# Hybrid encoder on one core: how the 64x64 triangular inverses are put together from 32x32 blocks

## The chip, the cores and the metric

The kernel runs on one core of one Trainium2 chip. The metric is the device time of one execution in microseconds (us). Three runs of the kernel before took 1709.49, 1710.0 and 1717.93 us, median 1710.0. The core has a matrix engine (TensorE; PE in the profile, its weight loads PEld), a vector engine (DVE), an activation engine (ScalarE, ACT), GpSimd (POOL) and SyncE (SP), which here issues DMAs.

## The reference

Two layers over 512 tokens of width 1024. Each layer normalises, projects, runs three token mixers beside each other, projects back, and ends with a gated MLP:

```
h = rms_norm(x);  proj = h @ w_in[l]
y_att = attention_mixer(...)     # windowed attention, 6 heads
y_dn  = deltanet_mixer(...)      # gated DeltaNet, two directions, 6 heads, chunks of 64
y_rw  = rwkv_mixer(...)          # RWKV-7, two directions, 4 heads
x = x + concat(y_att, y_dn, y_rw) @ w_out[l]
x = x + conv_ffn(rms_norm(x))
```

The change is in one piece of the two recurrent mixers. In DeltaNet, each chunk of 64 tokens needs the solution with a unit triangular matrix:

```
a_mat = lower + eye(64)          # strictly lower part from k_beta k^T * decay
sol = triangular_solve(a_mat, rhs, lower=True, unit_diagonal=True)
```

The reverse direction gives an upper triangle. RWKV-7 is written in the reference as a scan over tokens; the kernel computes it in chunks of 64 as well, with a unit triangular matrix per chunk and head. The kernel forms the inverses themselves. With 64 = 32 + 32 rows, the inverse of a block triangle has the inverses of the two diagonal blocks on its diagonal, and beside them one coupling block: inverse of one diagonal block, times the coupling block of the matrix, times the inverse of the other, with a sign.

## The kernel before

All matrix work is float32 through the matrix engine. A large projection splits both operands into a high and a low part and does three products for each weight tile of 128x128 (lines 332, 333, 334, each 128x512); the raw tile comes by DMA (`wr`, line 318), ACT makes its high part (`wh`, line 321), POOL its low part (`wl`, line 322). The weights stream in once per layer through three buffers of each.

A scheduler builds every engine's queue: the program is written as generators, each step carries costs and due times, and the rows of the queues differ from the order of the code. Each engine then works through its queue in order. The large products 332 to 334 are laid between the small products of the mixers as fillers. The order is not written by hand, so an edit in one helper shifts fillers in other places.

`invert` and `invert_both` (from lines 391 and 422) compute the inverses of all 32x32 diagonal blocks on DVE, four blocks of 32 partitions at a time, and leave them in two tiles: `o1`, and its transpose `o2`, each with one 32x32 block per unit. A unit is one chunk of one head pair; partitions 0 to 63 and 64 to 127 hold the two members `h` of the pair.

`finish_inverse` (line 445) then completes the 64x64 matrices `mt[h..h+64, c, 0:64]`, where before its call one off-diagonal block holds the coupling. It is called once per layer for RWKV (line 1005, 32 units, in groups of 16) and twice per layer for DeltaNet (line 1036, 24 units each, groups of 16 and 8). In a group:

- line 455: product `py`, coupling block (32x32, the weights) times `o2`, two products per unit (h = 0, 64), into PSUM;
- line 457: two ACT copies of 32 partitions, PSUM to the tile `yt`;
- line 461: product `pw`, `yt` block (32x32, the weights) times `o1`;
- line 465: per 8 units two ACT copies of 32 partitions from PSUM into the off-diagonal blocks, with the sign;
- line 469: per 8 units four ACT copies of 32 partitions put `o1` on the diagonal.

A float32 product shows as two matmul records in the trace: 64 products of lines 455 and 461 each in RWKV and 96 each in DeltaNet per layer give 256 and 384 records of the two lines together. The matrices are read next by the scans: line 619 (RWKV) and line 806 (DeltaNet), with 64x64 weights. Around them stand DeltaNet's conv lines 691 to 696, attention's products 886, 903 and 907, the rotary step line 867 on DVE, and the transposes 410 and 411, which write `o1` and `o2`. At the kernel's start `late_params` issues on SP the late part of the constants (line 205, 128x1816), and POOL makes its first low parts (line 322).

Of the kernel before, what the change touches and what calls it, by code (L numbers as in the profile page):

```python
# [7 lines left out]
F32 = mybir.dt.float32  # L8
F32R = mybir.dt.float32r
I32 = mybir.dt.int32  # L10
AF = mybir.ActivationFunctionType
# [3 lines left out]
P = 128  # L15
# [21 lines left out]
def _const_array():  # L37

    cols = []

    def add(name, a):
        a = np.asarray(a, np.float32)
        full = np.zeros((P, a.shape[1]), np.float32)
        full[: a.shape[0]] = a
        at = sum(c.shape[1] for c in cols)
        CONSTS[name] = (at, a.shape[1])
        cols.append(full)

    i = np.arange(P)
    add("ones", np.ones((P, P)))  # L50
    freq = np.zeros((P, 1))
    inv = (np.float32(500000.0) ** (-np.arange(8, dtype=np.float32) / np.float32(8))).astype(np.float32)
    for h in (0, 64):
        freq[h : h + 8, 0] = inv
        freq[h + 8 : h + 16, 0] = inv
    add("freq", freq)
    add("absign", np.where(np.arange(24) < 12, 1.0, -1.0)[:, None])
    for name, v in (("eps", EPS), ("rweps", RW_EPS), ("one", 1.0), ("halfpi", math.pi / 2)):
        add(name, np.full((P, 1), v))
    hi32 = (i % 64 >= 32).astype(np.float32)  # L60
    add("m32", np.stack([hi32 - 1.0, -hi32], 1))
    add("ident", np.eye(P))
    add("bd1", (i[:, None] // 64 == i[None, :] // 64))
    rot = np.zeros((P, P))
    for h in (0, 64):
        for d in range(8):
            rot[h + d + 8, h + d] = -1.0
            rot[h + d, h + d + 8] = 1.0
    add("rot", rot)
    kk = np.arange(384)  # L70
    add("attm", np.where(np.abs(kk[None, :] - 128 - i[:, None]) <= 128, 0.0, NEG))
    s, t = (i % 64)[:, None], np.arange(64)[None, :]
    add("mb", -np.concatenate([s < t, s <= t], 1).astype(np.float32))
    add("mkf", np.concatenate([s < t, s <= t], 1))
    add("mkb", np.concatenate([s > 63 - t, s >= 63 - t], 1))
    add("dnm", np.concatenate([np.where(s <= t, 0.0, NEG), np.where(s >= t, 0.0, NEG)], 1))
    add("smask", np.repeat((np.arange(T) % CL != 0)[None], P, 0))
    sel = np.zeros((P, 24))
    for hh in range(2):
        for p in range(3):  # L80
            for d in range(2):
                n, head = hh * 12 + p * 2 + d, p * 2 + hh
                sel[32 * d + 6 * d + head, n] = -1.0
                sel[64 + 12 + 6 * d + head, n] = 1.0
                sel[32 * d + 6 * d + head, n + 6] = -1.0
    add("sel", sel)
    return np.concatenate(cols, 1)


_CONST = _const_array()  # L90


# [23 lines left out]
def trunk(tc, t, out):  # L116
    nc = tc.nc
    V, S, G, PE = nc.vector, nc.scalar, nc.gpsimd, nc.tensor
    mult, add, sub, mx, mn = ALU.mult, ALU.add, ALU.subtract, ALU.max, ALU.min
    ctx = ExitStack()  # L120
    cp = ctx.enter_context(tc.tile_pool(name="cp", bufs=1))
# [5 lines left out]
    def nm(s):  # L127
        uid[0] += 1
        return f"{s}{uid[0]}"
# [5 lines left out]
    def ps(stream, shape=(P, T)):  # L135
        return psp.tile(list(shape), F32, tag="ps" + stream, bufs=PS_BUFS[stream], name=nm("ps"))
# [4 lines left out]
    def t2(stream, *free, dt=F32):  # L141
        return bp.tile([P, *(free or (T,))], dt, tag="t" + stream, bufs=T_BUFS[stream], name=nm("t" + stream))
# [31 lines left out]
    def C(name):  # L174
        a, n = CONSTS[name]
        return cst[:, a : a + n]

    ident, bd1, ones = C("ident"), C("bd1"), C("ones")
# [24 lines left out]

    def late_params():
        nc.sync.dma_start(cst[:, n0:], t["consts"][:, n0:])
        nc.sync.dma_start(par_all[:, :, n1:], t["params"][:, :, n1:])
        for l in range(DEPTH):
            nc.sync.dma_start(sinkb[l], t["attn_sink"][l].unsqueeze(0).broadcast_to([P, 6]))
# [22 lines left out]
    exp_ln_tables()  # L231

    pair_sq = cp.tile([P, 2, 32, 32], F32, name="pair_sq")


    cos_t, sin_t = fixed[:, W + DEPTH * NPAR : W + DEPTH * NPAR + T], fixed[:, W + DEPTH * NPAR + T : W + DEPTH * NPAR + 2 * T]
# [207 lines left out]

    def finish_inverse(st, o1, o2, units, upper, sign):

        ra, rb = (0, 32) if upper else (32, 0)
        n = len(units)
        for g0 in range(0, n, 16):
            grp = units[g0 : g0 + 16]  # L450
            py = ps(st)
            yt = t2(st, 16, 32)
            for i, (p, mt, c) in enumerate(grp):
                for h in (0, 64):
                    PE.matmul(py[h + rb : h + rb + 32, 32 * i : 32 * i + 32], mt[h + ra : h + ra + 32, c, rb : rb + 32], o2[h + ra : h + ra + 32, p, :], start=True, stop=True)  # L455
            for h in (0, 64):
                S.activation(yt[h + rb : h + rb + 32, : len(grp), :], py[h + rb : h + rb + 32, : 32 * len(grp)].rearrange("q (p c) -> q p c", c=32), AF.Copy)
            pw = ps(st)
            for i, (p, mt, c) in enumerate(grp):
                for h in (0, 64):  # L460
                    PE.matmul(pw[h + ra : h + ra + 32, 32 * i : 32 * i + 32], yt[h + rb : h + rb + 32, i, :], o1[h + rb : h + rb + 32, p, :], start=True, stop=True)  # L461
            for i in range(0, len(grp), 8):
                mt = grp[i][1]
                for h in (0, 64):
                    S.activation(mt[h + ra : h + ra + 32, :, rb : rb + 32], pw[h + ra : h + ra + 32, 32 * i : 32 * i + 256].rearrange("q (p c) -> q p c", c=32), AF.Copy, scale=sign)
        for i in range(0, n, 8):
            p, mt, _ = units[i]
            for h in range(0, P, 32):
                S.activation(mt[h : h + 32, :, h % 64 : h % 64 + 32], o1[h : h + 32, p : p + 8, :], AF.Copy)


    def token_shift(l, o, i, rb, dst):
# [439 lines left out]
    def layer(l, norm, xd, last):  # L912
# [9 lines left out]
        for i in range(8):  # L922
            o = proj(l, parts, COL_RW + P * i)
            if i == 0 and l == 0:
                derive_params()
            token_shift(l, o, i, rb, rkv[i // 2][:, i % 2, :])
            if i == 2 and l == 0:
                late_params()
            if i == 3:
                wau = bp.tile([P, 2, 256], F32, tag="wau", name=nm("wau"))  # L930
                nc.sync.dma_start(wau[0:64], t["rw_w_up"][l].rearrange("d r c -> r d c"))
                nc.sync.dma_start(wau[64:128], t["rw_a_up"][l].rearrange("d r c -> r d c"))
                gup = bp.tile([P, T], F32, tag="gup", name=nm("gup"))[:, :256]
                nc.sync.dma_start(gup, t["rw_g_up"][l])
# [68 lines left out]
        qkv.append(dn_proj(1))  # L1003
        o1, o2 = run(invert(rw["dpk"], True, V, t2("r")))
        finish_inverse("r", o1, o2, [(8 * u + c, rw["gb"][u], c) for u in range(4) for c in range(NCH)], True, 1.0)
        ap = attn_proj()
        heads = []
# [27 lines left out]
        for d in range(2):  # L1035
            finish_inverse("d", *inv[d], [(8 * p + c, dn["rm"][p][d], c) for p in range(3) for c in range(NCH)], d == 0, -1.0)
# [115 lines left out]
```

## Time and profile before

| | |
|---|---|
| runs of the kernel before | 1709.49, 1710.0, 1717.93 us |
| profiled execution, its own time | 1722.8 us |
| its span in the trace | 1721.0 us |
| mean granted TensorE clock | 0.931 |
| busy PE / PEld / DVE / ACT / POOL | 90 / 70 / 57 / 46 / 37% |
| copies of lines 457, 465, 469 | 24, 40, 80 |

The span is what the trace covers, from the first to the last instruction; 1.8 us of the execution's time lie around it. The profiled execution took 12.8 us more than the median of the three runs. A busy PE is counted from modelled ends of its instructions, which overlap, so the distance between two starts is the better price of a small product. The granted clock is given in parts of full speed, 1.0 for 2.4 GHz and 0.50 for 1.2 GHz.

### The profile page before, as it was taken

How to read it: one execution, taken by the hardware profiler on the slowest of the kernel's cores; microseconds unless marked ns; L12 is line 12 of the kernel's file. 1: busy time of each engine (PE TensorE's matmuls, PEld its weight loads, DVE VectorE, ACT ScalarE, POOL GpSimd, SP SyncE). 2: the span in 40 equal slices, each digit the busy share in tenths (PEclk: the TensorE clock that was granted, in tenths of full speed). 3: DMA queues.
4: the chain of work that ended last, by engine and by line, in shares of the span. 5: the costliest groups of instructions: out<-in, count | busy, mean ns of one | idle time of the engine just before them, and what ended most of it. 6: DMA issues, size and time to landing. Idle time of an engine off the chain costs nothing. (4 is left out here: it accounts for less than half of the span.)

```text
span 1721.0 us, 29049 instructions
## 1 busy us (share of the span) xinstructions
PE 1544.2 (90%) x11500; PEld 1208.7 (70%) x11500; DVE 973.5 (57%) x1595; ACT 792.0 (46%) x1493; POOL 638.7 (37%) x510
## 2 busy tenths in 40 slices
PE   7988889569999999999998887983899999999997
PEld 4676666347778888888876666652677788888885
DVE  6578946875535557731136797579563555555001
ACT  5547453355444444433336654351734544444321
POOL 4321323101265554445552112420104555555553
PEclk9989979669999999999999998995799999999998
DMA  6221211100143333333442012220003333333331
GB/s 185 73 57 38 56 38 44 37 2 20 36 122 96 98 98 95 96 104 114 119 101 68 25 45 50 55 70 1 4 19 93 102 95 97 98 99 114 101 101 65
DMA packets 230536, 126.07 MB, mean 73 GB/s; under 512 B 23656, under 2 KB 221416, under 8 KB 230400
## 3 DMA queue, kind: packets, MB, share of 16 engines
q1 hardware_dynamic: 228624, 121.02, 25.0%
q10 hardware_dynamic: 1776, 3.20, 0.6%
q8 instruction: 90, 1.47, 0.3%
q14 instruction: 46, 0.38, 0.1%
HBM read 117.84 MB, written 6.34 MB: 72 GB/s over the span
## 5 line engine op out<-in xcount | busy, mean ns | idle before, releaser
L322 POOL TENSOR_TENSOR wl<-wr,wh 128x512 fp32r<-128x512 f32 (+1 forms) x408 | 553.6, 1363 | 753.2 <-ACT wh L321 664.2
L332 PE MATMUL ps<-hh,wh 128*128 128x512 f32 x1248 | 505.2, 405 | 22.1 <-ACT wh L321 19.6
L333 PE MATMUL ps<-hl,wh 128*128 128x512 f32 x1248 | 504.5, 404 | 0.0
L334 PE MATMUL ps<-hh,wl 128*128 128x512 f32 x1248 | 500.9, 401 | 0.4 <-POOL wl L322 0.4
L321 ACT ACTIVATE wh<-wr 128x512 fp32r<-128x512 f32 (+1 forms) x408 | 246.2, 615 | 330.8 <-PE ps L333 262.4
L332 PEld LDWEIGHTS ps<-hh,wh 128*128 128x128 f32 x1248 | 237.8, 191 | 80.9 <-ACT wh L321 20.4
L333 PEld LDWEIGHTS ps<-hl,wh 128*128 128x128 f32 x1248 | 238.0, 191 | 56.8 <-issue 4.2
L334 PEld LDWEIGHTS ps<-hh,wl 128*128 128x128 f32 x1248 | 237.5, 190 | 56.8 <-issue 3.9
L1104 DVE TENSOR_TENSOR p<-ps,p 128x512 f32<-128x512 f32 x16 | 11.1, 692 | 196.6 <-PE ps L334 196.6
L332 PE MATMUL ps<-p,wh 128*128 128x512 f32 x256 | 99.6, 389 | 0.0
L333 PE MATMUL ps<-p,wh 128*128 128x512 f32 x256 | 99.6, 389 | 0.0
L334 PE MATMUL ps<-p,wl 128*128 128x512 f32 x256 | 99.6, 389 | 0.0
L903 PE MATMUL ps<-fixed,cv 128*128 128x128 f32 x120 | 24.9, 340 | 62.4 <-DVE cv L900 62.0
L1081 DVE TENSOR_TENSOR tr<-ps,rb 128x512 f32<-128x512 f32 x44 | 30.4, 691 | 80.9 <-PE ps L334 80.8
L292 POOL TENSOR_TENSOR tr<-tr,tr 128x512 f32<-128x512 f32 x32 | 42.6, 1332 | 70.4 <-ACT tr L285 59.9
L903 PEld LDWEIGHTS ps<-fixed,cv 128*128 128x128 f32 x120 | 16.0, 168 | 72.5 <-issue 44.8
L1084 DVE SCALAR_TENSOR_TENSOR td<-tr,fixed,td 128x511 f32<-128x511 f32 x44 | 42.8, 972 | 37.7 <-ACT td L1083 37.7
L285 ACT ACTIVATE tr<-p 128x512 f32<-128x512 f32 x36 | 22.6, 628 | 85.9 <-DVE p L1104 64.4
L791 POOL TENSOR_TENSOR sm<-sm,fixed 128x384 f32<-128x384 f32 x12 | 10.8, 896 | 121.5 <-DVE sm L820 64.5
L333 PEld LDWEIGHTS ps<-p,wh 128*128 128x128 f32 x256 | 48.1, 188 | 10.1
L332 PEld LDWEIGHTS ps<-p,wh 128*128 128x128 f32 x256 | 48.1, 188 | 10.1
L1084 DVE SCALAR_TENSOR_TENSOR tr<-td,fixed,tr 128x511 f32<-128x511 f32 x44 | 33.9, 771 | 37.5 <-ACT tr L1083 37.5
(294 smaller groups left out, 2559.7 us busy)
## 6 DMA issues: line engine op xcount, KB each, us to landing
wr<-ffn_w_up SPq DMA_DIRECT2D x176, 256.0 KB, 2.8
wr<-w_in SPq DMA_DIRECT2D x88, 256.0 KB, 2.9
wr<-ffn_w_down SPq DMA_DIRECT2D x80, 256.0 KB, 2.9
wr<-w_in SPq DMA_DIRECT2D x24, 128.0 KB, 2.4
p<-scr ACTq DMA_DIRECT2D x12, 256.0 KB, 3.5
wr<-w_out SPq DMA_DIRECT2D x32, 96.0 KB, 2.6
wr<-w_out SPq DMA_DIRECT2D x16, 192.0 KB, 2.9
p<-xt SPq DMA_DIRECT2D x8, 256.0 KB, 5.0
```

The source lines that it names most:

```text
L285: S.activation(sq, xk, AF.Square)
L292: G.tensor_tensor(acc, self.acc, sq, add)
L321: S.activation(hi[:, :n, :], raw[:, :n, :], AF.Copy)
L322: G.tensor_tensor(lo[:, :n, :], raw[:, :n, :], hi[:, :n, :].bitcast(F32), sub)
L332: PE.matmul(o, wh, xh, start=k == 0, stop=False)
L333: PE.matmul(o, wh, xl, start=False, stop=False)
L334: PE.matmul(o, wl, xh, start=False, stop=k == n - 1)
L791: G.tensor_tensor(gs, state, flat(gl, step), mult)
L903: PE.transpose(pp[:, P * j : P * j + P], scs[g][:, P * j : P * j + P], ident)
L1081: V.tensor_tensor(u, o, nf.rb, mult)
L1084: V.scalar_tensor_tensor(a[:, 1:], u[:, :-1], w(0), a[:, 1:], mult, add)
L1104: V.tensor_tensor(x1[j], o, x1[j], add)
```

## The change

The two products of a unit get weights of 64 columns in place of 32, so that each writes 64 partitions and its output lies on all 128 partitions for the pair. For `py` the weights are the whole rows of the coupling block, `mt[..., 0:64]`; the half of the output that comes from the other columns is not read. For `pw` the weights are `pair`: the block Y beside an identity block, so that the one product gives the whole block column (Y part times `o1`, and `o1` itself beside it). Y lies in a new tile `fin` (128 partitions, 33 blocks of 32), its odd slots; the even slots hold identities, written once by four POOL copies in `late_params`. The copies then go over all 128 partitions: one per group from `py` to `fin` with the sign, and per 8 units one of `o1` with a mask per partition (two more columns of the constant `m32`, zero on one half) and one of `pw`. `fin` is one tile for all groups, both mixers and both layers. Lines after the edit are 3 or 4 higher: 332 to 334 are 336 to 338, 867 is 870.

```
-    add("m32", np.stack([hi32 - 1.0, -hi32], 1))
+    add("m32", np.stack([hi32 - 1.0, -hi32, 1.0 - hi32, hi32], 1))
...
         nc.sync.dma_start(cst[:, n0:], t["consts"][:, n0:])
+        for h in range(0, P, 32):
+            G.tensor_copy(fin[h : h + 32, 0::2, :], ident[h : h + 32, h : h + 32].unsqueeze(1).broadcast_to([32, 17, 32]))
...
+    fin = cp.tile([P, 33, 32], F32, name="fin")
...
+        mask = C("m32")[:, 2 + ra // 32 : 3 + ra // 32]
...
+            s0 = 0
             py = ps(st)
-            yt = t2(st, 16, 32)
...
-                    PE.matmul(py[h + rb : h + rb + 32, 32 * i : 32 * i + 32], mt[h + ra : h + ra + 32, c, rb : rb + 32], o2[h + ra : h + ra + 32, p, :], start=True, stop=True)
-            for h in (0, 64):
-                S.activation(yt[h + rb : h + rb + 32, : len(grp), :], py[h + rb : h + rb + 32, : 32 * len(grp)].rearrange("q (p c) -> q p c", c=32), AF.Copy)
+                    PE.matmul(py[h : h + 64, 32 * i : 32 * i + 32], mt[h + ra : h + ra + 32, c, 0:64], o2[h + ra : h + ra + 32, p, :], start=True, stop=True)
+            S.activation(fin[:, 2 * s0 + 1 : 2 * (s0 + len(grp)) : 2, :], py[:, : 32 * len(grp)].rearrange("q (p c) -> q p c", c=32), AF.Copy, scale=sign)
             pw = ps(st)
             for i, (p, mt, c) in enumerate(grp):
+                at_i = 2 * (s0 + i) + (0 if upper else -1)
+                pair = fin.rearrange("p a b -> p (a b)")[:, 32 * at_i + 32 : 32 * at_i + 96]
                 for h in (0, 64):
-                    PE.matmul(pw[h + ra : h + ra + 32, 32 * i : 32 * i + 32], yt[h + rb : h + rb + 32, i, :], o1[h + rb : h + rb + 32, p, :], start=True, stop=True)
+                    PE.matmul(pw[h : h + 64, 32 * i : 32 * i + 32], pair[h + rb : h + rb + 32, :], o1[h + rb : h + rb + 32, p, :], start=True, stop=True)
             for i in range(0, len(grp), 8):
-                mt = grp[i][1]
-                for h in (0, 64):
-                    S.activation(mt[h + ra : h + ra + 32, :, rb : rb + 32], pw[h + ra : h + ra + 32, 32 * i : 32 * i + 256].rearrange("q (p c) -> q p c", c=32), AF.Copy, scale=sign)
-        for i in range(0, n, 8):
-            p, mt, _ = units[i]
-            for h in range(0, P, 32):
-                S.activation(mt[h : h + 32, :, h % 64 : h % 64 + 32], o1[h : h + 32, p : p + 8, :], AF.Copy)
+                p, mt, _ = grp[i]
+                S.activation(mt[:, :, ra : ra + 32], o1[:, p : p + 8, :], AF.Copy, scale=mask)
+                S.activation(mt[:, :, rb : rb + 32], pw[:, 32 * i : 32 * i + 256].rearrange("q (p c) -> q p c", c=32), AF.Copy)
```

New lines: `py` 461, its copy 462, `pw` 468, the masked copy of `o1` 471, the copy of `pw` 472, the identities 207. The scheduler lays some instructions otherwise than before, here at three places.

PE's queue before, layer 1, where RWKV's inverses are completed (`p_621`, `p_646`, `p_1160`, `p_1185` are the four matrix tiles `mt`):

```order
L334 MATMUL ps_2247<-hh_143,wl_2257 128x512
L455 MATMUL ps_1618<-p_1615,p_621 32x32 x16
L455 MATMUL ps_1618<-p_1615,p_646 32x32 x16
L461 MATMUL ps_1654<-p_1614,tr_1619 32x32
L455 MATMUL ps_1691<-p_1615,p_1160 32x32 x16
L455 MATMUL ps_1691<-p_1615,p_1185 32x32 x5
L461 MATMUL ps_1654<-p_1614,tr_1619 32x32 x31
L455 MATMUL ps_1691<-p_1615,p_1185 32x32 x11
L461 MATMUL ps_1727<-p_1614,tr_1692 32x32
```

The same place in the changed kernel:

```order
L338 MATMUL ps_2334<-hh_98,wl_2339 128x512
L461 MATMUL ps_1623<-p_1620,p_626 64x32 x16
L461 MATMUL ps_1623<-p_1620,p_651 64x32 x16
L336 MATMUL ps_2334<-hh_108,wh_2338 128x512
L337 MATMUL ps_2334<-hl_109,wh_2338 128x512
L338 MATMUL ps_2334<-hh_108,wl_2339 128x512
L336 MATMUL ps_2334<-hh_114,wh_2338 128x512
L337 MATMUL ps_2334<-hl_115,wh_2338 128x512
L338 MATMUL ps_2334<-hh_114,wl_2339 128x512
L336 MATMUL ps_2334<-hh_123,wh_2345 128x512
L468 MATMUL ps_1657<-p_1619,fin 64x32 x32
L461 MATMUL ps_1694<-p_1620,p_1165 64x32 x16
```

Six products of the next projection (`ps_2334`) stand ahead of the first `py`, seven between the first `py` and the first `pw`, and four between the second pair; before there were none. When the scan's first step (line 619, now 622) is through, 19 of them are done in place of 11.

DVE's queue before, at the same place (`tr_2184` is the rotary step on the projection's result, which frees its PSUM buffer):

```order
L404 TENSOR_TENSOR p_1551<-p_1551,tr_1550 128x2x29
L403 TENSOR_TENSOR tr_1550<-p_1551 128x30
L404 TENSOR_TENSOR p_1551<-p_1551,tr_1550 128x30
L410 STREAM_TRANSPOSE p_1614<-p_1551 128x32x32
L411 STREAM_TRANSPOSE p_1615<-p_1551 128x32x32
L867 SCALAR_TENSOR_TENSOR tr_2184<-ps_2146,rb_88 128x512
```

In the changed kernel the rotary step stands ahead of the last steps of the inverse:

```order
L408 TENSOR_TENSOR p_1556<-p_1556,tr_1555 128x7x24
L870 SCALAR_TENSOR_TENSOR tr_2169<-ps_2131,rb_89 128x512
L407 TENSOR_TENSOR tr_1555<-p_1556 128x150
L699 TENSOR_TENSOR cv_2012<-cv_2012,td_2020 128x512
L408 TENSOR_TENSOR p_1556<-p_1556,tr_1555 128x6x25
```

So the buffer that the six fillers write is free before the transposes, and the transposes come one instruction later.

PE's queue before, layer 1, where DeltaNet's inverses are completed (the second direction, `p_1881`, `p_2691`, `p_2780`):

```order
L461 MATMUL ps_3305<-p_3141,td_3270 32x32 x31
L455 MATMUL ps_3342<-p_3142,p_2780 32x32 x16
L334 MATMUL ps_3620<-hh_97,wl_3624 128x512
L332 MATMUL ps_3620<-hh_107,wh_3623 128x512
L333 MATMUL ps_3620<-hl_108,wh_3623 128x512
L334 MATMUL ps_3620<-hh_107,wl_3624 128x512
L461 MATMUL ps_3362<-p_3141,td_3343 32x32
L332 MATMUL ps_3620<-hh_113,wh_3623 128x512
L461 MATMUL ps_3362<-p_3141,td_3343 32x32 x15
L806 MATMUL ps_3439<-p_1921,p_1880 64x64 x2
```

And in the changed kernel:

```order
L468 MATMUL ps_3272<-p_3126,fin 64x32 x32
L461 MATMUL ps_3309<-p_3127,p_2765 64x32 x16
L338 MATMUL ps_3573<-hh_92,wl_3577 128x512
L336 MATMUL ps_3573<-hh_98,wh_3576 128x512
L337 MATMUL ps_3573<-hl_99,wh_3576 128x512
L338 MATMUL ps_3573<-hh_98,wl_3577 128x512
L468 MATMUL ps_3327<-p_3126,fin 64x32 x16
L809 MATMUL ps_3392<-p_1906,p_1865 64x64 x2
```

From the first `py` to the end of the scan's first step there were 12 fillers and are now 6; the small pieces of one kind set between two fillers, or fillers set singly into a row of small products, go from 6 to 3. In RWKV they go from 4 to 5.

At the start of the program SP issues the late constants behind three loads of raw weights in place of six, and POOL's queue is, after the change:

```order
L326 TENSOR_TENSOR wl_165<-wr_83,wh_164 128x512
L326 TENSOR_TENSOR wl_217<-wr_214,wh_216 128x512
L207 COPY fin<-fixed 32x17x32 x4
L326 TENSOR_TENSOR wl_223<-wr_220,wh_222 128x512
L326 TENSOR_TENSOR wl_259<-wr_256,wh_258 128x512
```

The four copies of identities stand between the third and the fourth weight's low part; before, nothing stood there.

## Rows read from the trace of the kernel before

**Rows 1.** The page: busy time by engine, and PE's granted clock over 40 slices.

```profile
PE 1544.2 (90%) x11500; PEld 1208.7 (70%) x11500; DVE 973.5 (57%) x1595; ACT 792.0 (46%) x1493; POOL 638.7 (37%) x510
PEclk9989979669999999999999998995799999999998
```

**Rows 2.** Stretches: start:end, us; busy us of PE, PEld, DVE, ACT, POOL; clock; DMA.

```profile
220.00:228.70 8.70, 6.16 (x201) 5.71 (x201) 1.24 (x3) 6.21 (x14) 0.00 (x0) 0.50 0.01 4
228.70:238.10 9.40, 9.40 (x85) 6.09 (x84) 0.00 (x0) 5.89 (x15) 1.27 (x1) 0.50 0.08 28
238.10:310.00 71.90, 70.74 (x852) 49.16 (x853) 48.42 (x83) 30.00 (x61) 27.36 (x31) 0.99 0.21 59
368.80:391.70 22.90, 21.04 (x437) 15.96 (x437) 6.80 (x15) 19.30 (x48) 0.00 (x0) 0.65 0.01 3
391.70:440.00 48.30, 45.55 (x807) 35.70 (x808) 31.78 (x100) 23.74 (x67) 8.37 (x8) 0.98 0.07 18
```

**Rows 3.** PE's timeline, RWKV: start, us, instruction, [idle before, releaser].

```profile
211.06 0.39 PE L333 MATMUL ps<-hl,wh 128*128 128x512 f32 x1
211.28 0.39 PE L334 MATMUL ps<-hh,wl 128*128 128x512 f32 x1
220.07 1.92 PE L455 MATMUL ps<-p,p 32*32 32x32 f32 x64 [8.40 <-DVE p L411]
222.68 0.26 PE L461 MATMUL ps<-p,tr 32*32 32x32 f32 x1 [0.69 <-ACT tr L457]
227.82 0.31 PE L461 MATMUL ps<-p,tr 32*32 32x32 f32 x2 [1.78 <-ACT tr L457]
...
232.66 0.63 PE L332 MATMUL ps<-hh,wh 128*128 128x512 f32 x1
233.09 0.63 PE L333 MATMUL ps<-hl,wh 128*128 128x512 f32 x1
233.65 0.48 PE L619 MATMUL ps<-p,p 64*64 64x64 f32 x4
234.06 0.79 PE L334 MATMUL ps<-hh,wl 128*128 128x512 f32 x1
234.65 0.63 PE L332 MATMUL ps<-hh,wh 128*128 128x512 f32 x1
```

**Rows 4.** PE's timeline, DeltaNet's inverses and scan.

```profile
379.12 1.20 PE L455 MATMUL ps<-p,p 32*32 32x32 f32 x63
388.56 1.54 PE L806 MATMUL ps<-p,p 64*64 64x64 f32 x22
...
407.32 0.92 PE L806 MATMUL ps<-sm,p 64*64 64x64 f32 x24 [0.67 <-DVE sm L802]
408.97 0.82 PE L903 MATMUL ps<-fixed,cv 128*128 128x128 f32 x6
410.10 1.25 PE L907 MATMUL ps<-tr,at 128*64 128x128 f32 x12
```

**Rows 5.** PE's timeline, a product with 12 moving columns.

```profile
112.82 0.61 PE L723 MATMUL ps<-fixed,td 128*64 128x12 f32 x14 [1.23 <-DVE td L367]
```

**Rows 6.** DVE's timeline, end of RWKV's 32x32 inverses.

```profile
218.13 1.89 DVE L411 STREAM_TRANSPOSE p<-p 128x1024 f32<-128x1024 f32 x1
219.90 0.65 DVE L867 SCALAR_TENSOR_TENSOR tr<-ps,rb 128x512 f32<-128x512 f32 x1
```

**Rows 7.** Groups by line, ACT: count | busy us, mean ns | idle before, releasers.

```profile
L469 ACT ACTIVATE p<-p 32x256 f32<-32x256 f32 x80 | 33.1, 414 | 17.9 <-DVE p L410 13.8 <-DVE p L440 3.0
L465 ACT ACTIVATE p<-ps 32x256 f32<-32x256 f32 x40 | 15.0, 375 | 5.1 <-PE ps L461 4.2
```

**Rows 8.** Start of the program: POOL's and PE's timeline.

```profile
19.11 2.86 POOL L322 TENSOR_TENSOR wl<-wr,wh 128x512 fp32r<-128x512 f32 x2
23.26 1.31 POOL L322 TENSOR_TENSOR wl<-wr,wh 128x512 fp32r<-128x512 f32 x1 [1.29 <-DMA wr<-w_in]
...
31.41 0.39 PE L334 MATMUL ps<-hh,wl 128*128 128x512 f32 x1
```

## The prediction

> **What bounds the kernel now.** I read the page first. PE is busy 90% of the span, ACT 46%, and the clock row stands at 9 in most slices, with dips in those where the mixers' small products run [rows 1]. Then the windows around the edit, in layer 1 [rows 2]. In the two stretches that follow the inverses, PE is busy 70.74 of 71.9 us and 45.55 of 48.3 us: whatever ACT saves there, PE has no gaps from which it could be paid back. The inverses' own stretches look different. RWKV's, 220.0 to 228.7, has PE at 6.16 of 8.70 us and ACT at 6.21, at clock 0.50. DeltaNet's, 368.8 to 391.7, has PE at 21.04 of 22.90 and ACT at 19.30, at 0.65. Last I read PE's timeline in those stretches for what ends each wait [rows 3]: 8.40 us on the DVE transpose, then 0.69 and 1.78 us on the ACT copies from `py`. So only two things count: PE time added or taken, and these few idle microseconds.
>
> **ACT's copies.** Before, 24 copies of line 457, 40 of 465 and 80 of 469. The last two cost 15.0 and 33.1 us [rows 7], and line 457 about 24 x 0.5 = 12 us more (its width is up to twice that of line 465's 0.375 us). After: 12, 20 and 20 copies of all partitions, at most 0.5 us each by the same rows (an ACT copy is priced there by its width, 0.375 to 0.414 us for 256), together about 24 us. ACT sheds some 36 us in the program. I put this at nothing by itself: it is off the path, apart from the waits counted below.
>
> **The products.** Their number is unchanged, 256 records per layer in RWKV and 384 in DeltaNet. Each now loads 64 weight columns in place of 32 and moves 32 as before. The price is the interval between starts. 32x32: (1.92 - 0.24) / 63 = 26.7 ns at clock 0.50 [rows 3], (1.20 - 0.19) / 62 = 16.3 ns at full clock [rows 4]. The trace has no 64x32. The bounds are unchanged (26.7 and 16.3), and 64x64: (1.54 - 0.32) / 21 = 58 ns slow, about 30 ns fast ((0.92 - 0.2) / 23 = 31) [rows 4]. To choose between them I looked for what the price follows. Fast, the 128*64 with 128 moving columns costs (1.25 - 0.28) / 11 = 88 ns, the 128*128 with 128 moving (0.82 - 0.26) / 5 = 112 ns [rows 4]: 0.46 and 0.44 ns for each column, loaded and moved together. Where products alternate between two row groups, as here (h = 0, 64), it is half: 32 + 32 gives 14 (measured 16.3), 64 + 64 gives 29 (about 30). By that 64 + 32 costs 1.5 times the old, 40 ns slow and 24.5 fast. RWKV runs slow: 256 x 13.3 = 3.4 us. DeltaNet about half and half: 384 x (13.3 + 8.2) / 2 = 4.1 us. Together **+7.5 us a layer**.
>
> The Trainium skill, "TensorE: Matmul & The Clock Gate", section "LDWEIGHTS (loading the stationary operand)", says that a load takes time by its number of columns, not of rows: 64 columns would take twice what 32 do. It speaks against the change, and by it alone the sum would be that of the second rival below, not this one. The trace agrees in part: a 128*64 product that moves only 12 columns still costs (0.61 - 0.206) / 13 = 31 ns [rows 5], so the load does count, yet the rows above make it one of two terms.
>
> **Idle time that goes.** RWKV's two waits on copies, 0.69 + 1.78 [rows 3], have fillers in them now. In DeltaNet's stretch PE is idle 22.90 - 21.04 = 1.86 us [rows 2]. Late next is the copy into `fin` in DeltaNet's first group, where `pw` follows `py` with no filler between: one full copy and its semaphores, which I put at 0.9 us (line 457's waits of 0.69 and 1.78 stand on both sides of it). 0.69 + 1.78 + 1.86 - 0.9 = **-3.4 us a layer**. Bounds: 0 if new waits eat it all, -4.3 if none appears. `fin` is one tile, so the second group's copy waits for the first group's `pw`; in PE's order that `pw` comes before the second `py` is through, so nothing is queued behind it.
>
> **Six fillers in the gap before RWKV's first `py`.** They go where PE sits idle 8.40 us, and cost nothing there; elsewhere they were 6 x 0.22 us, the distance of lines 333 and 334 [rows 3], 1.3 us. For it the rotary step, 0.65 us [rows 6], runs ahead of DVE's last steps and delays the transposes, on which `py` waits. 0.65 - 1.3 = **-0.65 us a layer**.
>
> **Small pieces between fillers.** A small piece set between two fillers costs more than its own time. From 233.09: 0.56 to the piece, 0.41 from it, 0.59 to the next filler [rows 3], against 2 x 0.43 for the fillers alone and 4 x 0.058 for the piece: 1.56 - 0.86 - 0.23 = 0.47 us. RWKV has one more (+0.47), DeltaNet three fewer (-1.4): **-0.9 us a layer**.
>
> **Fillers between clocks.** A filler takes 0.43 us at 0.50 [rows 3] and 0.22 at full clock. RWKV does 19 - 11 - 6 = 2 more in the slow stretch (+0.4), DeltaNet 6 fewer, half of them slow (-0.6): **-0.2 us a layer**.
>
> **The start.** Four copies on POOL stand ahead of the fourth low part. The first use of such a part that could be late is at 31.41 us, and it takes 1.31, so it must begin by 30.1; POOL ends the third at 21.97 [rows 8]. The 8.1 us between are 2.0 for each copy; the nearest row is the low part itself, 2.86 / 2 = 1.43 us for 512 columns (a copy has 544). I take 0, hidden behind products that are already fed. The constants now go ahead of the raw weights of the later parts; with 7.1 us of delay the slack would be used up, so the bounds are 0 and 2 us, once.
>
> **Sum.** 7.5 - 3.4 - 0.65 - 0.9 - 0.2 = +2.35 us a layer, +4.7 in two (layer 2 repeats the stages). The profiled execution took 1722.8 us (span 1721.0 and 1.8 around it) and would take 1727.5. The runs' median is 12.8 lower: 1727.5 - 12.8 = 1714.7, forecast **1715**.
>
> **Rivals.**
> (a) The wider load hides fully, and the price stays at 26.7 and 16.3. For it: loads of PE run beside products, PEld is busy 70% [rows 1]. Against it: rows 4 and 5, where loaded columns count. Then 2.35 - 7.5 = -5.15 a layer, -10.3 in two: 1700.
> (b) The 64-column load sets the pace, as if the product were 64x64. RWKV 256 x 31.3 = 8.0, DeltaNet 384 x (31.3 + 13.7) / 2 = 8.6, together 16.6 in place of 7.5: +11.45 a layer, +22.9: 1733. It is slower, and decides from about 43 ns a record at the slow clock (the sum's 40 and 3.8 us in two layers). For it: row 5's 31 ns with 12 columns moving. Against it: those weights have 128 rows and follow each other on the same rows.
> (c) The clock in DeltaNet. A mean of 0.65 in 22.90 us [rows 2] is about 30% at full clock, 6.9 us, with PE at 0.92 of it. With six fillers fewer the full-clock part may not come: 6.3 us a layer more, 1715 + 12.6 = 1728.
> (d) The clock in RWKV the other way. It was 0.50 from the first `py` on, after 8.40 us of idle. With six fillers in the gap, and eleven standing among the inverses' products where none stood, it may rise sooner: half of the 18.1 us from 220.0 to 238.1 [rows 2] is 9, of which I take 7, since waits don't shrink; 1715 - 14 = 1701.
> (e) The saved ACT time counts in full where ACT set the pace in the inverses' stretches: ACT 6.21 of 8.70 and 19.30 of 22.90. The idle time above is all that PE could win by it, so this is in the sum already.
>
> **How the numbers follow.** A measurement of this kernel can tell about 0.5%, 8.5 us: faster is below 1701.5, slower above 1718.5. Forecast (1705 to 1722): 0.46. (a) 0.23, (b) 0.16, (c) 0.08, (d) 0.07. Below 1701.5 lie most of (a) and half of (d), and little of the forecast: 0.27. Above 1718.5 lie (b), (c) and an edge of the forecast: 0.29. Between: 0.44. The range goes from just under (a) to just under (b), 1697 to 1731, which leaves out half of (b) and the tails; the forecast's own range is 1705 to 1722.
>
> **What would show it.** In the profile after: records of lines 461 and 468 at about 40 ns from start to start in RWKV (27 speaks for (a), 58 for (b)). ACT's lines 462, 471 and 472 at 24 us together. PE's idle before the first `pw` in RWKV gone, and the wait for DVE's transposes below 8.40. DeltaNet's first `pw` waiting about 0.9 us for its copy. POOL's low parts at the start late with no PE wait behind them. PE busy as before in the stretches after the inverses. The prediction is wrong if PE's total changes by more than 10 us either way, or if a stage that this edit does not touch moves because the scheduler laid its fillers otherwise.

## The result and the profile after

The changed kernel took 1736.97 us (median of 4 runs, 1736.14 to 1745.58), the kernel before, run beside it, 1710.28. The ratio is 1.0154, 95% interval 1.0117 to 1.0192: slower by 1.5%, some 26 us, clear of no change. The forecast was 1715 us, with a range up to 1731. In all comparisons the kernel before came out between 1709 and 1728 us, so below only ratios to runs on the same chip are compared, and stretches within a trace.

The profiled execution took 1736.1 us, its span was 1734.3. The page's busy times and clock row, as [rows 1] showed them before:

```profile
PE 1569.1 (90%) x11500; PEld 1237.0 (71%) x11500; DVE 964.0 (56%) x1595; ACT 754.8 (44%) x1401; POOL 646.0 (37%) x514
PEclk9999979659999999999999897995699999999998
```

ACT lost 37.2 us and 92 instructions, as forecast (36 and 92). PE gained 24.9 us with the same number of instructions; more than 10 was named as a sign of being wrong. Which stretch holds them is seen from windows over the two places where inverses are completed, in layer 1: the wait before RWKV's first `py`, from there to the scan's first product, a stretch further on, and DeltaNet's first `py` to its scan's first product. Columns: start:end, us; busy us of PE, PEld, DVE, ACT, POOL (instructions); granted clock; DMA share and GB/s. The changed kernel:

```profile
208.56:216.13 7.57, 0.00 (x0) 0.00 (x0) 7.16 (x13) 0.00 (x0) 1.49 (x3) 0.59 0.00 1
216.13:232.38 16.25, 16.25 (x268) 14.10 (x268) 5.11 (x7) 6.05 (x14) 1.28 (x1) 0.61 0.07 18
240.00:310.00 70.00, 68.08 (x832) 47.55 (x830) 46.22 (x83) 27.93 (x57) 25.66 (x29) 1.00 0.19 54
363.00:392.90 29.90, 29.19 (x406) 24.82 (x406) 8.26 (x16) 12.38 (x31) 0.00 (x0) 0.50 0.01 2
```

The kernel before, the two windows that end at the scan's first product, which [rows 2] cut otherwise:

```profile
220.00:228.00 8.00, 5.46 (x194) 5.19 (x194) 1.24 (x3) 5.54 (x13) 0.00 (x0) 0.50 0.02 4
368.80:388.50 19.70, 17.84 (x410) 13.71 (x410) 6.80 (x14) 16.37 (x42) 0.00 (x0) 0.67 0.01 3
```

RWKV's window is now full (PE busy 16.25 of 16.25 us): it holds eleven fillers that stood later before, so its length says little by itself. From the first RWKV `py` to the first DeltaNet `py` there are 148.7 us before and 146.9 after (layer 2: 148.9 and 149.2), and PE is busy in 109.7 and 111.2 of them: it has gaps there. DeltaNet's window is the one that lost. It grew from 19.7 to 29.9 us with four fillers fewer in it (six fewer up to the end of the scan's first step), and its clock is 0.50 throughout, where it was 0.67. In layer 2 it grew by the same, 10.1 us (scan start after first `py`: 19.8, then 29.9). RWKV's window in layer 2 ran at 0.50 throughout and took 18.98 us.

PE's timeline of the changed kernel at these places (start, us, instruction, idle before and its releaser):

```profile
208.17 0.39 PE L338 MATMUL ps<-hh,wl 128*128 128x512 f32 x1
216.13 3.62 PE L461 MATMUL ps<-p,p 32*64 32x32 f32 x64 [7.58 <-DVE p L415]
219.69 0.80 PE L336 MATMUL ps<-hh,wh 128*128 128x512 f32 x1
...
225.08 1.86 PE L461 MATMUL ps<-p,p 32*64 32x32 f32 x58
...
363.02 3.62 PE L461 MATMUL ps<-p,p 32*64 32x32 f32 x64 [3.66 <-DVE nmx L895]
367.33 3.31 PE L468 MATMUL ps<-p,fin 32*64 32x32 f32 x58 [0.69 <-ACT fin L462]
...
374.31 1.12 PE L910 MATMUL ps<-tr,at 128*64 128x128 f32 x4
...
382.62 1.65 PE L889 MATMUL ps<-at,at 64*128 64x384 f32 x4
...
392.92 1.54 PE L809 MATMUL ps<-p,p 64*64 64x64 f32 x24
```

The row to read first is `x64`: the same 64 records that took 1.92 us [rows 3] take 3.62. From start to start that is (3.62 - 0.29) / 63 = 52.9 ns at the slow clock; at full clock (1.86 - 0.22) / 57 = 28.8 ns. The prediction had 40 and 24.5, between bounds of 26.7 and 58 slow.

ACT's new copies, by form: count | busy us, mean ns | idle before, releasers. The group of the 8 wide copies into `fin` is shown; the four of 8 units have 384 ns each.

```profile
L471 ACT ACTIVATE p<-p,fixed 128x256 f32<-128x256 f32 x20 | 9.8, 501 | 3.8 <-PE ps L461 3.7
L472 ACT ACTIVATE p<-ps 128x256 f32<-128x256 f32 x20 | 6.8, 381 | 31.5 <-PE ps L468 31.5
L462 ACT ACTIVATE fin<-ps 128x512 f32<-128x512 f32 x8 | 4.8, 598 | 31.6 <-PE ps L461 31.6
```

About 23 us together. ACT now waits 31 us in the program for each of the two products. The longest of these waits, 13.2 us, counts time in which PE itself still waits for DVE's transposes.

### The profile page after: what moved, and what is told of

The parts are those of the page before. It is cut to its first block, busy times and chain, and to the rows that moved or that the text cites. A ratio compares the mean times of both kernels' runs of the same rounds, so it can differ in the third digit from the quotient of the medians.

```text
span 1734.3 us, 28973 instructions
## 1 busy us (share of the span) xinstructions
PE 1569.1 (90%) x11500; PEld 1237.0 (71%) x11500; DVE 964.0 (56%) x1595; ACT 754.8 (44%) x1401; POOL 646.0 (37%) x514
## 5 line engine op out<-in xcount | busy, mean ns | idle before, releaser
L296 POOL TENSOR_TENSOR tr<-tr,tr 128x512 f32<-128x512 f32 x32 | 42.9, 1342 | 54.6 <-ACT tr L289 44.4
L794 POOL TENSOR_TENSOR sm<-sm,fixed 128x384 f32<-128x384 f32 x12 | 10.1, 842 | 142.1 <-DVE sm L823 81.8
L461 PE MATMUL ps<-p,p 32*64 32x32 f32 x640 | 36.3, 283 | 22.4 <-DVE p L415 15.1
L337 PEld LDWEIGHTS ps<-p,wh 128*128 128x128 f32 x256 | 48.1, 188 | 10.8
L338 PEld LDWEIGHTS ps<-p,wl 128*128 128x128 f32 x256 | 48.0, 188 | 10.8
```

The lines of the kernel that those rows point to most:

```text
L296: G.tensor_tensor(acc, self.acc, sq, add)
L337: PE.matmul(o, wh, xl, start=False, stop=False)
L338: PE.matmul(o, wl, xh, start=False, stop=k == n - 1)
L461: PE.matmul(py[h : h + 64, 32 * i : 32 * i + 32], mt[h + ra : h + ra + 32, c, 0:64], o2[h + ra : h + ra + 32, p, :], start=True, stop=True)
```

## The experiments

**The kernel before once more.** Its profiled execution had taken 12.8 us more than its median, so a second profile was taken.

> The unchanged kernel once more, for a second profile of it. The profiled execution of the kernel before took 1722.8 us, 12.8 above its median, while that of the changed kernel took 1736.1, 0.8 below its median. If the extra time is lost ahead of the mixers (the slow clock stretches before 200 us), this profile has the first record of line 455 near 214 to 216 us in place of 220.07 and a time near 1710. If it comes near 1723 with 220 again, the profile before is the ordinary one and the changed kernel's start is really 3.9 us faster.

1714.0 us, span 1712.1, and the first record of line 455 at 215.4. The front of the program held 4.7 us of the first profile's extra time, and the changed kernel's start (216.1) is no faster. From RWKV's first `py` to DeltaNet's there are 146.9 us, as in the changed kernel; from DeltaNet's first `py` to the same product of the output projection 92.3 (95.7 in the first profile, 105.1 in the changed kernel). The windows from DeltaNet's first `py` to the scan, layers 1 and 2:

```profile
362.31:380.85 18.54, 16.18 (x410) 12.48 (x410) 6.80 (x14) 16.40 (x42) 0.00 (x0) 0.77 0.01 3
1199.70:1222.52 22.82, 21.84 (x410) 16.40 (x410) 6.80 (x14) 16.41 (x42) 0.00 (x0) 0.50 0.01 2
```

So the kernel before takes 18.5 to 22.8 us here, with the clock that it happens to be granted. Where both kernels run at 0.50, the window is 29.9 - 22.8 = 7.1 us longer after the change.

**The wide loads alone.**

```
-  PE.matmul(py[h + rb : ...], mt[h + ra : ..., c, rb : rb + 32], o2[...])
+  PE.matmul(py[h : h + 64, ...], mt[h + ra : ..., c, 0:64], o2[...])
-  PE.matmul(pw[h + ra : ...], yt[h + rb : ..., i, :], o1[...])
+  PE.matmul(pw[h : h + 64, ...], yt(flat)[h + rb : ..., 32 * i - ra : 32 * i - ra + 64], o1[...])
```

> The kernel before with 64 weight columns in both products, copies as before (the wider half of each output is not read; the unit at a group's edge keeps 32). Theory 1, the load sets the pace by its columns: 53 ns a record at clock 0.50 and 27 at full clock, RWKV +256 x 0.94 x 26 = 6.3 us a layer, DeltaNet 384 x 0.92 x 31 = 11 if all of it runs slow: 1710 + 2 x 17 = 1744, slower than the changed kernel, which has the copies' waits shorter. Theory 2, loaded and moved columns add up as in the prediction: 40 and 24.5 ns, about 1725. Theory 3, the loss of the changed kernel comes from its order and the tile fin: 1710 to 1713 here.

The unit at a group's edge keeps 32 columns. Ratio 1.0259 (1.0227 to 1.0291), 44 us. Theory 3 falls: the loads alone lose more than the whole change does. Theory 2 falls too (1.009 expected). Theory 1 had the price right and the time too low (34 us, 1.020). PE's timeline in this kernel, DeltaNet's first products:

```profile
375.99 3.62 PE L455 MATMUL ps<-p,p 32*64 32x32 f32 x64 [3.72 <-DVE nmx L896]
```

52.9 ns again, under the old copies. The order is not quite that of before: the window from there to the scan holds 13 fillers, where before it held 10 and in the changed kernel 6.

```profile
375.99:412.81 36.82, 35.94 (x413) 28.33 (x414) 7.58 (x15) 19.35 (x47) 0.00 (x0) 0.50 0.01 2
```

**Wide moving operand, narrow loads.**

```
+  m = min(64, 32 * len(grp) - 32 * i)
-  PE.matmul(py[..., 32 * i : 32 * i + 32], mt[..., rb : rb + 32], o2[..., p, :])
+  PE.matmul(py[..., 32 * i : 32 * i + m], mt[..., rb : rb + 32], o2[..., p : p + m // 32, :])
```

(`pw` likewise.)

> The kernel before with 32 weight columns and 64 moving columns in both products (the second 32 are the neighbour's block, overwritten by the next product). Theory 1, the load sets the pace: the interval stays at 26.7 ns slow and 16 fast, and the time within 0.5% of 1710. Theory 2, loaded and moved columns add up: 40 and 24.5 ns, 7.5 us a layer, 1725.

Ratio 1.0187 (1.0158 to 1.0216). Both theories missed. The price was neither unchanged nor 40 ns:

```profile
367.97 3.51 PE L456 MATMUL ps<-p,p 32*32 32x64 f32 x64 [3.65 <-DVE nmx L894]
```

The last record has 32 moving columns and takes 0.24: (3.51 - 0.24) / 63 = 51.9 ns. So at the slow clock 32 loaded and 32 moved cost 26.7 ns, 64 and 32 cost 52.9, 32 and 64 cost 51.9. For 64 and 64 the prediction read 58 from a row of 22 records [rows 4]; the changed kernel's row of 24 (line 809 above) gives (1.54 - 0.31) / 23 = 53.5. These numbers are neither a sum nor the load alone: the larger of the two counts sets the pace, and the smaller adds next to nothing. The products here alternate between two row groups; that the one group's load runs under the other's product would give this, and was not tried by itself.

**Fewer copies, narrow products.**

```
-  four copies of o1 of 32 partitions per 8 units
+  for a in (ra, rb):
+      S.activation(mt[:, :, a : a + 32], o1[:, p : p + 8, :], AF.Copy, scale=mask of a)
```

> The kernel before with products of 32 columns as they were, and the diagonal blocks written by two masked copies over all partitions in place of four copies of 32 partitions, 40 instead of 80. ACT sheds 33.1 us and gets 40 x 0.5 = 20. The prediction's step (ACT off the path) says 1708 to 1711, no change. The rival, that ACT's copies set the pace in the inverses' stretches, says that PE's idle of 2.5 us in RWKV and 1.9 in DeltaNet goes in part: 1702 to 1706.

Ratio 0.9964 (0.9944 to 0.9984): 0.4% faster, 6 us, a small gain that is clear of no change and less than a single run can tell. Of 1710 us that is 1704: in the rival's range, and below that of the prediction's step. But the idle time that the rival wanted gone is still there: PE idles 2.53 us before RWKV's scan (2.47 before) and 0.98 in DeltaNet's window, which ran at 0.50 in both layers here (0.98 at that clock before). From RWKV's first `py` to DeltaNet's there are 144.3 and 145.7 us in the two layers, where the two profiles of before had 146.9 to 149.1; what shortened them is not shown.

**DeltaNet narrow, RWKV as changed.** The kernel after, with the old `finish_inverse` for DeltaNet.

```
-  finish_inverse("d", *inv[d], ...)
+  finish_narrow("d", *inv[d], ...)     # the old function
```

> The changed kernel with DeltaNet's inverses completed as before (products of 32 columns, its copies too), RWKV's as changed. The loss by stage: in the trace of the changed kernel DeltaNet's products to the scan's start take 10 us more a layer and RWKV's stretch up to there nothing. Theory 1 (the wide products' price and the clock under them, in DeltaNet): 1.000 to 1.003 of before, near no change. Rival (the tile fin, the order or RWKV carry it): 1.010 or more.

Ratio 1.0020 (0.9994 to 1.0047), as theory 1 said. Windows of this kernel, RWKV's and DeltaNet's inverses:

```profile
216.60:232.90 16.30, 16.30 (x269) 14.13 (x271) 5.05 (x7) 6.09 (x15) 1.27 (x1) 0.60 0.07 18
363.40:383.00 19.60, 17.21 (x420) 13.26 (x422) 6.83 (x14) 16.63 (x43) 0.00 (x0) 0.74 0.01 3
```

RWKV's is that of the changed kernel, DeltaNet's that of the kernel before, and with it the loss is gone.

**RWKV narrow, DeltaNet as changed**, the other half.

> The changed kernel with RWKV's inverses completed as before and DeltaNet's as changed: the other half of the run that had DeltaNet narrow (1.002). If the loss is DeltaNet's wide loads at the slow clock (inverses 29.9 us in place of 19.7): 1.011 to 1.015. If the two halves only lose together: 1.005 or less.

Ratio 1.0112 (1.0077 to 1.0148): the loss stays. Window of DeltaNet's inverses:

```profile
366.70:396.60 29.90, 29.21 (x408) 24.80 (x408) 8.17 (x16) 12.32 (x31) 0.00 (x0) 0.50 0.01 2
```

The two halves add up within their intervals: 0.2 and 1.1%, against 1.5%.

**Narrow products in the changed kernel.** The identity half comes from one float32 product per group.

```
+  PE.matmul(pw[:, : 32 * len(grp)], ident, o1[:, g0 : g0 + len(grp), :], start=True, stop=True)
-  PE.matmul(pw[h : h + 64, ...], pair[h + rb : h + rb + 32, :], o1[...])
+  PE.matmul(pw[h + ra : h + ra + 32, ...], pair[h + rb : h + rb + 32, ra : ra + 32], o1[...])
```

(`py` back to 32 columns, its copy in two halves.)

> The changed kernel with products of 32 columns; what the identity half of the pair gave comes from one product per group, identity 128x128 times o1, laid into the bank ahead of the narrow ones; the copy into fin goes in two halves of 32 partitions. Copies of o1 and of the block column as changed. Theory 1 (the pace is the larger of columns loaded and moved, 53 or 27 ns slow): 17 us a layer less for the products and some 6 us more for five wide float32 products, so 1.002 to 1.005 of before, and up to 1% less if the fewer copies gain as much as the difference between the changed kernel (1.015) and the wide loads alone (1.026) says. Rival (the order decides): still 1.010 or more.

Ratio 1.0042 (1.0019 to 1.0064), where theory 1 put it. One such product is dear at the slow clock, 2.0 us to the next start, and stands in for the second half of 64 loads:

```profile
221.74 1.92 PE L461 MATMUL ps<-p,p 32*32 32x32 f32 x64 [7.63 <-DVE p L415]
223.59 2.08 PE L465 MATMUL ps<-p,fixed 128*128 128x512 f32 x2
```

**Wide loads in RWKV alone, in the old order.** The kernel before, with wide loads and the old copies in a second `finish_inverse` for RWKV.

> The kernel before with wide loads in RWKV alone, copies as before. In the changed kernel RWKV's wide loads cost nearly nothing (1.002 with DeltaNet narrow). If what pays for them there is the order of the fillers and the waits they fill: here 7 to 8 us a layer, 1.008 to 1.010. If wide loads are hidden in RWKV in any order: 1.000 to 1.003.

Ratio 1.0095 (1.0063 to 1.0127), as expected for the order, where the same loads under the changed kernel cost 0.2%. From RWKV's first `py` to DeltaNet's there are 154.2 and 153.7 us, in the changed kernel 146.9 and 149.2. The window shows the two waits on copies still open, 15.79 busy of 17.20 us, at the slow clock throughout, where layer 1 of the changed kernel has 16.25 of 16.25 and 0.61:

```profile
221.10:238.30 17.20, 15.79 (x266) 14.65 (x266) 1.20 (x2) 9.23 (x21) 0.00 (x0) 0.50 0.01 2
```

**Wide loads with the masked copies.**

> The wide loads (1.026 of before alone) with the two masked copies of the diagonal in place of four. The changed kernel has wide loads too, 52 copies and another order, and stands at 1.015. If the number of ACT copies carries the difference: 1.018 to 1.021 (104 copies of 144 and 52). If the order and the tile fin carry it: 1.022 to 1.026, no more than the 0.4% that the masked copies gave with narrow products.

Ratio 1.0272 (1.0245 to 1.0299), no better than the wide loads alone. So 40 copies fewer give nothing here, and it is not by these that the changed kernel stands 1% below the wide loads. What is left is the order of the fillers, `fin`, which allows it, and the other 52 copies, those of `py` and `pw`; these can't be told apart by these runs.

**Feeding PE while it waits.** The narrow kernel with masked copies, and products whose result nobody reads in the steps of the 32x32 inverses:

```
+  def feed(src, n):
+      o, hi = ps("r"), hh tile 0
+      PE.matmul(o[0:2, 0:2], src, src, start=True, stop=True)
+      for _ in range(n):
+          PE.matmul(o, hi[:, 0:P], hi, start=True, stop=True)
...
+  feed(L[:, j + 1, 0:2], 3)            # RWKV, steps from 16
+  feed(L[:, 0, j + 1, 0:2], 5)         # DeltaNet, steps from 12
```

> The narrow kernel with masked copies (0.996 of before), and in the steps of the 32x32 inverses, where PE waits for DVE, products 128x512 whose result nobody reads: three a step in RWKV from step 16, five in DeltaNet from step 12, each tied to DVE's step by a product of 2 columns. Theory clock (the inverses' products run at 0.50 because PE idled before them): the clock rises to 1.0 in RWKV's inverses and scan start (18 us at 0.50 there, worth 7 to 9 us a layer) and in DeltaNet's (40 us at 0.50, worth 8 to 15): 0.975 to 0.99 of before. Rival (the small products themselves keep the clock low, or the added products delay the others): 0.996 to 1.01.

Ratio 1.0224 (1.0188 to 1.0261): worse than either range. The clock rose as the theory said (0.96 over the span, from 0.93), yet the time did not follow. RWKV's stretch:

```profile
205.00:240.00 35.00, 33.19 (x494) 23.95 (x493) 19.59 (x35) 14.64 (x31) 7.77 (x9) 1.00 0.13 32
```

Clock 1.00 all through, and RWKV's inverses took 8.0 us in place of 11.0 (from the first to the last of their records). In DeltaNet fed products stand on PE ahead of attention's, and DVE waits for attention's. Its first waits for them are those of the kernel without feeding (0.30 and 1.51 us in both); the later ones grow from 0.43 to 2.89, and from none to 7.96:

```profile
350.10 0.62 DVE L897 CUSTOM_DVE_ANT_0 cv<-ps,fixed 128x384 f32<-128x384 f32 x1 [2.89 <-PE ps L896]
...
360.21 0.22 DVE L443 TENSOR_TENSOR pair_sq<-pair_sq,cv 128x60 f32<-128x60 f32 x1
368.39 0.48 DVE L897 CUSTOM_DVE_ANT_0 cv<-ps,fixed 128x256 f32<-128x256 f32 x1 [7.96 <-PE ps L896]
```

PE at the same place:

```profile
358.88 1.43 PE L397 MATMUL ps<-hh 128*128 128x512 f32 x5
...
366.30 1.43 PE L397 MATMUL ps<-hh 128*128 128x512 f32 x5
367.65 0.70 PE L896 MATMUL ps<-at,at 64*128 64x256 f32 x4
```

DVE was through with its steps at 360.4 and then stood idle, while PE worked off six groups of fed products without a gap; only then came attention's. DeltaNet's first `py` came at 385.6, against 360.9 without feeding.

**Feeding in RWKV's gap alone**, three products a step from step 24, and eight each under the two transposes.

> The narrow kernel with masked copies; the unread products now only in RWKV's gap, three a step from step 24, eight after the last step and eight after the first transpose, none in DeltaNet. In the run with feeding everywhere RWKV's inverses took 8.0 us in place of 11.0 at clock 1.0, while DeltaNet's attention products queued behind the fed ones. Theory (the clock before the inverses costs, and what lost was the queueing in DeltaNet): RWKV's inverses 8.0 us, the clock 1.0 from 205 to 240, 4 to 8 us a layer gained: 0.987 to 0.992 of before. Rival (what the clock gives back is idle time in the scan, where ACT and DVE set the pace): 0.994 to 0.998, as the masked copies alone.

Ratio 0.9937 (0.9910 to 0.9964): faster than the kernel before, the best of all runs. Its interval overlaps that of the masked copies without feeding (0.9944 to 0.9984), so the part that feeding adds is not shown; the time lies between the two expected ranges, at the edge of the rival's. The windows before and from the first `py`:

```profile
206.00:220.19 14.19, 13.55 (x52) 8.08 (x52) 9.14 (x18) 2.75 (x6) 1.43 (x2) 0.76 0.11 37
220.19:229.20 9.01, 9.01 (x281) 7.38 (x280) 2.54 (x3) 7.58 (x18) 0.00 (x0) 1.00 0.01 4
```

The inverses run at full clock, 9.2 us to the end of their last record with 17 fillers among them, in place of 11.3 with two (216.61 to 227.91 without feeding). The price is that fed products themselves ran slow until about 213.8 and kept the first `py` waiting, which came 3.6 us later (220.19, from 216.61). From there to DeltaNet's first `py` feeding gains less than that, 1.4 us in layer 1 and 3.3 in layer 2 (142.9 and 142.4, from 144.3 and 145.7).

**Feeding in both, late.**

> As the one before, and in DeltaNet four unread products a step from step 27 and six after the first transpose. DeltaNet's inverses ran 19 to 22 us, of which up to 20 at 0.50. If the clock rises for them: 4 to 8 us a layer more, 0.980 to 0.988 of before. If the few steps don't raise it, or attention's products queue behind them: as the one before or up to 1% above it.

Ratio 1.0020 (0.9998 to 1.0042): 0.8% above the run before it, as the second case had it. In DeltaNet's inverses the clock is 0.85, but PE now idles 3.6 us there and the stretch is no shorter than without feeding at 0.50 (22.2):

```profile
366.60:388.80 22.20, 18.61 (x425) 13.61 (x423) 8.37 (x22) 17.15 (x42) 0.00 (x0) 0.85 0.01 3
```

## Why the prediction was wrong

**The products: the step that failed.** The step read "loaded and moved together" from the 128-column rows, halved it for two row groups, and got 1.5 times the old price. It agreed with 32/32 and 64/64, since where both counts are equal a sum and a maximum differ by a constant factor only. The trace of before had a row that tells them apart, line 594, whose products alternate between two row groups with 64 columns loaded and 128 moved, at clock 0.50 and at 1.00:

```profile
94.80 2.61 PE L594 MATMUL ps<-p,p 64*64 64x128 f32 x22 [4.25 <-DVE p L543]
...
154.41 5.46 PE L594 MATMUL ps<-p,p 64*64 64x128 f32 x96 [0.41 <-DVE p L547]
```

That is (2.61 - 0.42) / 21 = 104 ns slow and (5.46 - 0.27) / 95 = 54.6 fast. The halved sum gives 87 (1.5 times its 58) and 43. Beside 64/64 only the moved count doubled, and the price nearly doubled with it (from 53.5 and 31). The prediction did not look there. The runs put the maximum in the place of the sum: 52.9 ns slow and 28.8 fast, where it had 40 and 24.5. The rule of the Trainium skill ("TensorE: Matmul & The Clock Gate", section "LDWEIGHTS (loading the stationary operand)"), that a load's time goes by its columns, agrees with 26.7 and 52.9 ns at the slow clock; the run with 64 moving columns shows that it is one of two limits.

**The clock under them, the second part of the same term.** DeltaNet's records were priced half slow and half fast. All of them ran at 0.50. The term of 4.1 us a layer becomes 384 x (52.9 - 21.5) = 12.1 us, 8.0 more; the new price alone would have made it 7.4, the slow clock alone 7.1. Attention's products in the stretch ran slow as well: line 910 1.12 us a group where line 907 had 0.65, line 889 1.65 where line 886 had 0.92, about 2 us a layer. With layer 2 this makes 2 x (8.0 + 2) = 20 of the 22 us between forecast and result. How much of the clock part is the change's own stays open: in the second profile, layer 2 of the kernel before ran at 0.50 as well. In RWKV the price was too low, and in layer 1 the clock too pessimistic: the records from 223.5 to 226.9 ran fast, 28.8 ns, so that its 3.4 us came out at about 128 x 26.2 + 128 x 2.1 = 3.6. In layer 2 all ran slow, 256 x 26.2 = 6.7 us; as PE has gaps up to DeltaNet's first `py`, little of it shows there (149.2 us, from 148.9).

Rivals (b) and (c) had the two parts, the price of a 64x64 product and a slow DeltaNet; each was worked out with the other left at the forecast, and none stood for both at once. On the products (b) was right: the 64-column load did set the pace, at 52.9 ns where it took 58. What it left out is that 64 moving columns set the same pace.

**Did the wider loads also slow the clock?** From DeltaNet's first `py` to its scan, in the two layers of every profile: with 64 columns loaded or moved there, none of ten stretches got above 0.52. With narrow products and nothing fed there, seven of 14 ran wholly at 0.50 and seven at 0.67 to 0.77, and the same kernel did both (0.77 and 0.50 in the second profile of before). That wide products hold the clock down is likely by this count and not shown by a run of its own; that they pay more at the slow clock is shown (52.9 ns a record for 26.7, and 7.1 us in the window with four fillers fewer in it).

**Idle time.** Right. RWKV's two waits are gone (3.6 against 3.4 us saved a layer: 2.47, and in DeltaNet 1.86 - 0.71 = 1.15; 0.27 against the 0.98 that PE idled there where the kernel before ran at 0.50). The new wait for `fin` measured 0.69, put at 0.9.

**The gap, small pieces, fillers.** Right in direction: 8.40 became 7.58, and the six fillers ran ahead of it. Their sizes were too small in sum: the run with wide loads in RWKV in the old order lost 0.95%, the changed kernel's RWKV 0.2%, so that order, filled waits and fewer copies together give back about 0.75%, 13 us or 6 a layer in RWKV, where the steps had 2.47 + 0.65 - 0.47 - 0.4 = 2.25. Part of that is the clock in layer 1, 0.61 in place of 0.50.

**ACT.** Right in size, 37 us less, and nearly so in worth. The masked copies alone gained 0.4%, where the prediction had nothing; with wide loads they gained nothing.

**The start.** Right: the four copies take 2.69 us together, 0.67 each (priced 1.43), and no product waits for them:

```profile
21.45 2.69 POOL L207 COPY fin<-fixed 32x544 f32<-32x544 f32 x4
24.23 2.54 POOL L326 TENSOR_TENSOR wl<-wr,wh 128x512 fp32r<-128x512 f32 x2
```

## What to carry to other kernels

Before a copy is saved by a wider product, price the product by the interval between starts in the very pattern it will run in, and at the clock of that stretch; a row with equal loaded and moved counts can't tell whether they add or the larger rules, so look for one with unequal counts in the same pattern. Before a stretch's clock is put down to a change, read the same stretch in both layers and in a second profile. A saving on an engine that waits is worth the waits it ends and no more. Where two rivals share a stretch, work out the case in which both happen.

## What the runs showed of the hardware

For float32 products that alternate between two row groups the interval followed the larger of loaded and moved columns: 26.7 (32/32), 52.9 (64/32), 51.9 (32/64) and 53.5 ns (64/64) at 0.50; 16.3 (32/32), 28.8 (64/32), about 31 (64/64) and 54.6 (64/128) at 1.00. The granted clock stayed at 0.50 through a stretch in which PE was busy 29.19 of 29.90 us with such products, and in RWKV's stretch it stood at 1.00 from the first `py` on where 128x512 products had filled the wait before it; a clock that is raised this way shortens the stretch only as far as no other engine is waited for, as in DeltaNet at 0.85.
